# One row of condition, joined transposes and keys ahead of values in a hybrid convolution-attention layer on one core

## The chip, the cores and the metric

The kernel runs on one core of a Trainium2 chip. The metric is device time in microseconds (us) of one execution, as the median of several runs. A trace of one further execution, taken with the hardware profiler, shows what each engine did: PE (TensorE: matmuls; PEld are its weight loads), DVE (VectorE), ACT (ScalarE), POOL (GpSimd) and SP (SyncE, which here issues the DMAs).

## The reference

One layer for 512 latent tokens (a grid of 8 rows x 64 columns) and 256 context tokens, 1024 channels, all in fp32.

```python
sh, sc, gt = split(silu(c) @ w_mod + b_mod, 3)            # the condition's modulation
h  = rmsnorm(x, pre_g) * (1 + sc) + sh                    # latent tokens
hc = rmsnorm(ctx, pre_g) * (1 + sc_c) + sh_c              # context tokens, from c_ctx
b_gate, c_gate, x_in, z_a, q, k, v, z_b, g_a, g_b = split(h @ w_in)
k_c, v_c = split(hc @ w_in[:, keys and values])
q, k = rope(q), rope(k)                                   # 16 heads of 64
attn = softmax(q . [k in an 8 x 16 window, k_c] / 8 + bias) @ [v in the window, v_c]
y_a = (silu(z_a) * b_gate * conv3(c_gate * x_in)) @ w_out_conv
y_b = (silu(z_b) * attn) @ w_out_attn
y = (sigmoid(g_a) * y_a + sigmoid(g_b) * y_b) @ w_o
out = x + gt * rmsnorm(y, post_g)
```

## The kernel before, in words

Channels stand on partitions: a tensor of 512 tokens is eight tiles of 128 channels x 512 tokens. Every fp32 operand of a large matmul is split into a high and a low part (`split`, L67: ACT casts the high part, L70, DVE subtracts it from the source, L71), and a product is three matmuls, high x high, high x low, low x high (`step_T`, L115 to L117; `proj_N`, L128 and L132; `proj_c`, L140 and L144). Weights come in chunks (`Chunk`), are loaded by SP and split by ACT and DVE; the list `order` (L176) says in which order.

**The opening** (L316 to L409) is written out by hand: inside `manual_schedule` PE, DVE, ACT and SP keep the order of the code. SP loads the condition, broadcast to 128 partitions (`cb`, L317), four tiles of x (128 tokens x 1024), then per step k two slabs of the modulation weights (`wm`) and the first projection weights (`fraw`). ACT applies SiLU to `cb`. `square`, `root` and `norm` make the RMSNorm of each x tile; DVE squares tiles 0 and 1, ACT tiles 2 and 3; DVE scales tiles 0 to 2, ACT tile 3. `condition` (L260) multiplies a slab with `cb` and sums over it on DVE: half 0 gives the scale, half 1 the shift of 128 channels. PE meanwhile runs matmuls whose result nobody reads (`keep_busy`, L352) and transposes x into channels on partitions. In the loop over k (L379) ACT casts the weights (`cast_first`), DVE finishes the condition and the low part (`rest_first`), ACT modulates the transposed x (L390), `split` makes `hx`, and PE adds six projections at once (`steps`, L308 to L312).

**The middle.** After the opening a scheduler places the instructions of PE, DVE, ACT and SP, from the order of the code, the dependences, and its own estimate of durations. `turned` (L244) transposes the two context tiles for one k into a bank (banks 6 and 7 in turn) and ACT evacuates them. Convolution units follow, then `values(0)` and `keys_queries(0)` (L626). The latter projects queries and keys, applies `rope` on DVE, and writes the split operands `qd`, `qe` and `ks`. The former writes `V`.

**The attention loop** (L645) runs over 64 blocks (8 pairs of heads x 2 heads x 4 blocks of 128 queries), with projections for later pairs (`plan`, `fill`) strewn between. For block i it issues `scores` of block i + 2 (L534 or L543 on PE into bank 3 or 4; maximum with bias on DVE, L550; exponent on ACT, L557; scaling on DVE, L559, into `pt`, of which there are three buffers), then `turn` of block i: four transposes of `pt` (L565) into bank 5 or 6, and a `split` of the bank into `TH` and `TL`. After four blocks `gather` multiplies `TH` and `TL` with `V` (L580). The output stage (from L669) is not touched.

Of the kernel before, what the change touches and what calls it, by code (L numbers as in the profile page):

```python
# [9 lines left out]
F32 = mybir.dt.float32  # L10
# [17 lines left out]
def layer(ctx: ExitStack, tc, xp, ctxt, cc, wmod, small, wfirst, win, wout, wo, rel, tab, out):  # L28
# [147 lines left out]
    order = [win[i] for i in range(8)] + [vz(0, 0), qk(0)]  # L176
# [56 lines left out]
    with ExitStack() as p0:  # L233
# [10 lines left out]
        def turned(dst, xn, k):  # L244
            tp = tps()
            n = len(xn)
            for t in range(n):
                nc.tensor.transpose(tp[:, t * P:(t + 1) * P], xn[t][:, k * P:(k + 1) * P], ident)
            nc.scalar.activation(dst, tp[:, :n * P], AF.Identity, scale=sp[:, PG + k:PG + k + 1])
# [26 lines left out]

        bsc1 = const.tile([P, KT], F32, name="bsc1")
# [38 lines left out]
        with tc.manual_schedule(engines={E.PE, E.DVE, E.Activation, E.SP}):  # L316
            nc.sync.dma_start(cb[:, 0], cc[0:1].broadcast_to([P, D]))  # L317
# [6 lines left out]
            nc.vector.memset(eps, EPS)  # L324

            nc.scalar.activation(cb[:, 0], cb[:, 0], AF.Silu)
# [25 lines left out]
            def keep_busy(n, cols):  # L352

                for _ in range(n):
                    nc.tensor.matmul(acc[5][:, :cols], lhsT=ident, rhs=cb[:, 0, :cols], start=True, stop=True)

            square(0)
            square(1)
            root(0)
            norm(0)  # L360
            square(2)
            root(1)
            root(2)
            norm(1)
            norm(2)
            square(3)
            root(3)
            norm(3)
            nc.vector.tensor_scalar(out=bsc1, in0=sp[:, BM + 8:BM + 16], scalar1=1.0, scalar2=None, op0=ALU.add)
            nc.vector.tensor_scalar(out=hcv, in0=sp[:, CW:CW + 32], scalar1=0.5, scalar2=None, op0=ALU.mult)  # L370
            keep_busy(2, S)
            turned_x = {k: tps() for k in range(2)}
            for t in range(4):
                for k in range(2):
                    nc.tensor.transpose(turned_x[k][:, t * P:(t + 1) * P], xn[t][:, k * P:(k + 1) * P], ident)
                keep_busy(1, 256 if t < 3 else S)
            keep_busy(1, 256)

            for k in range(KT):  # L379
                cast_first(k)  # L380
                if k == 0:
                    condition(k, 0, [0])
                condition(k, 0, [1])
                col = cols.pop((k, 0))
                nc.vector.tensor_mul(col[:, 0:1], col[:, 0:1], sp[:, PG + k:PG + k + 1])
                rest_first(k)
                if k + 1 < KT:
                    condition(k + 1, 0, [0])
                m = st.tile([P, S], F32, name="m", bufs=2)
                nc.scalar.activation(m, turned_x.pop(k), AF.Identity, bias=col[:, 1:2], scale=col[:, 0:1])  # L390
                split(hx[0][k], hx[1][k], m)
                if k + 3 < KT:
                    load_slab(k + 3)
                    load_first(k + 3)
                elif k == 5:
                    after = Chunk(order[3])
                steps(k)
                if k + 2 < KT:
                    turned_x[k + 2] = turn_x(k + 2)
# [19 lines left out]
        for k in range(KT):  # L419
            turned(ctT[k], cn, k)  # L420
# [141 lines left out]
    def turn(pt, TH, TL):  # L562
        tp = psT().rearrange("p (c q) -> p c q", c=4)
        for c in range(4):
            nc.tensor.transpose(tp[:, c], pt[:, c * P:(c + 1) * P], ident)  # L565
        split(TH, TL, tp)
# [59 lines left out]
    for g in (values(0), keys_queries(0)):  # L626
# [15 lines left out]
    pts = {i: scores(*blocks[i]) for i in range(2)}  # L642
    T = None
    done = 0
    for i, (p, h, b) in enumerate(blocks):  # L645
# [16 lines left out]
        turn(pts.pop(i), TH[:, b], TL[:, b])  # L662
# [193 lines left out]
```

## Time and profile before

| | |
|---|---|
| median of 3 runs | 734.83 us (734.79 to 734.86) |
| the profiled execution | 737.3 us, of which the span is 733.0 us |
| PE busy | 717.9 us, 98% |
| PE weight loads busy | 598.9 us, 82% |
| DVE busy | 513.7 us, 70% |
| ACT busy | 335.1 us, 46% |
| chain that ended last | PE 94%, DVE 2%, DMA 1%, ACT 1% |
| moved by DMA | 86.09 MB, mean 117 GB/s; 344 and 405 GB/s in the first two of 40 slices |

The span is the time from the first to the last instruction; the rest of an execution lies around it. A row of the timeline has start, length, engine, line, operation, tiles (out<-in), shapes and a count, and in brackets the idle time of the engine just before, with what ended it. A matmul's row is longer than the time that it holds PE, since matmuls are pipelined: the pitch is read from one start to the next. An fp32 matmul leaves two records, an fp32r one or a transpose leaves one.

### The profile page before, as it was taken

How to read it: one execution, taken by the hardware profiler on the slowest of the kernel's cores; microseconds unless marked ns; L12 is line 12 of the kernel's file. 1: busy time of each engine (PE TensorE's matmuls, PEld its weight loads, DVE VectorE, ACT ScalarE, POOL GpSimd, SP SyncE). 2: the span in 40 equal slices, each digit the busy share in tenths (PEclk: the TensorE clock that was granted, in tenths of full speed). 3: DMA queues.
4: the chain of work that ended last, by engine and by line, in shares of the span. 5: the costliest groups of instructions: out<-in, count | busy, mean ns of one | idle time of the engine just before them, and what ended most of it. 6: DMA issues, size and time to landing. Idle time of an engine off the chain costs nothing.

```text
span 733.0 us, 9376 instructions
## 1 busy us (share of the span) xinstructions
PE 717.9 (98%) x3518; PEld 598.9 (82%) x3518; DVE 513.7 (70%) x1056; ACT 335.1 (46%) x617; POOL 0.7 (0%) x6
## 2 busy tenths in 40 slices
PE   5999999999999999999999999999999999999996
PEld 2887888788888888888888888888888888888886
DVE  6979998897897968869879778676753223234423
ACT  6575524463465544644546545534722223314321
POOL 0000000000000000000000000000000000000000
PEclk9999999999999999999999999999999999999999
DMA  9976783213122132122221212222132232234503
GB/s 344 405 264 208 278 282 114 87 44 129 58 73 72 40 104 67 65 72 72 94 94 45 93 65 72 78 81 87 58 114 83 90 115 88 85 115 147 197 1 114
DMA packets 25820, 86.09 MB, mean 117 GB/s; under 512 B 2992, under 2 KB 3376, under 8 KB 25776
## 3 DMA queue, kind: packets, MB, share of 16 engines
q1 hardware_dynamic: 25632, 85.31, 33.6%
q8 instruction: 27, 0.44, 0.2%
q10 hardware_dynamic: 144, 0.20, 0.1%
q14 instruction: 17, 0.14, 0.1%
HBM read 83.40 MB, written 2.10 MB: 117 GB/s over the span
## 4 chain that ended last, share of the span: by engine, by line
PE 94%; DVE 2%; DMA 1%; ACT 1%; issue 1%; SPq 0%; DVEq 0%; ACTq 0%
PE ps L115 20%; PE ps L116 20%; PE ps L117 20%; PE ps L128 6%; PE ps L733 6%; PE ps L580 4%; PE ps L565 4%; PE ps L132 3%; PE ps L534 3%; PE ps L308 2%; PE ps L140 2%; PE ps L309 2%; PE ps L312 1%; PE ps L543 1%; DMA x<-in_xp 1%; PE ps L144 1%
## 5 line engine op out<-in xcount | busy, mean ns | idle before, releaser
L115 PE MATMUL ps<-h,w 128*128 128x512 f32 x528 | 210.0, 398 | 0.0
L116 PE MATMUL ps<-h,w 128*128 128x512 f32 x528 | 206.2, 391 | 0.0
L117 PE MATMUL ps<-h,w 128*128 128x512 f32 x528 | 205.9, 390 | 0.0
L71 DVE TENSOR_TENSOR w<-raw,w 128x1024 fp32r<-128x1024 f32 (+1 forms) x98 | 113.4, 1173 | 61.5 <-ACT w L70 61.3
L70 ACT CAST w<-raw 128x1024 fp32r<-128x1024 f32 (+1 forms) x98 | 97.1, 1016 | 85.1 <-PE ps L117 62.8
L117 PEld LDWEIGHTS ps<-h,w 128*128 128x128 f32 x528 | 99.2, 188 | 21.3
L115 PEld LDWEIGHTS ps<-h,w 128*128 128x128 f32 x528 | 99.2, 188 | 19.6
L116 PEld LDWEIGHTS ps<-h,w 128*128 128x128 f32 x528 | 99.3, 188 | 19.2
L557 ACT ACTIVATE pt<-ps,m 128x512 f32<-128x512 f32 x64 | 44.1, 690 | 36.8 <-DVE m L554 35.8
L550 DVE CUSTOM_DVE_ANT_1 ps<-ps,bt 128x512 f32<-128x512 f32 x56 | 38.8, 695 | 17.0 <-PE ps L534 13.8
L71 DVE TENSOR_TENSOR TL<-ps,TH 128x512 fp32r<-128x512 f32 x64 | 43.5, 682 | 5.4 <-ACT TH L70 4.5
L128 PE MATMUL ps<-w,h 128*128 128x512 f32 x128 | 45.6, 398 | 0.0
L70 ACT CAST TH<-ps 128x512 fp32r<-128x512 f32 x64 | 37.1, 586 | 18.0 <-PE ps L565 17.5
L693 DVE SCALAR_TENSOR_TENSOR g<-g,ps 128x512 f32<-128x512 f32 x16 | 11.0, 686 | 39.2 <-PE ps L117 39.1
L565 PE MATMUL ps<-ident,pt 128*128 128x128 f32 x256 | 38.2, 272 | 0.0
L613 ACT ACTIVATE g<-ps 128x512 f32<-128x512 f32 x16 | 9.6, 598 | 60.3 <-PE ps L117 60.3
L565 PEld LDWEIGHTS ps<-ident,pt 128*128 128x128 f32 x256 | 31.1, 140 | 6.2 <-DVE pt L559 0.2
L132 PE MATMUL ps<-w,h 128*128 128x256 f32 x128 | 36.0, 281 | 0.0
L559 DVE TENSOR_SCALAR pt<-pt,z 128x512 f32<-128x512 f32 x64 | 30.8, 483 | 1.1
L499 ACT ACTIVATE qd<-ta 64x512 fp32r<-64x512 f32 x32 | 20.2, 631 | 18.6 <-PE ps L543 10.9
L580 PE MATMUL ps<-TH,V 128*128 128x256 f32 (+1 forms) x96 | 28.5, 319 | 0.0
L128 PEld LDWEIGHTS ps<-w,h 128*128 128x128 f32 x128 | 24.0, 188 | 5.2
(152 smaller groups left out, 1186.2 us busy)
## 6 DMA issues: line engine op xcount, KB each, us to landing
raw<-in_win SPq DMA_DIRECT2D x74, 512.0 KB, 4.1
wm<-in_wmod SPq DMA_DIRECT2D x34, 512.0 KB, 6.3
raw<-in_wout SPq DMA_DIRECT2D x16, 512.0 KB, 4.1
bt<-in_rel SPq DMA_DIRECT2D x16, 256.0 KB, 2.6
raw<-in_wo SPq DMA_DIRECT2D x8, 512.0 KB, 4.8
fraw<-in_wfirst SPq DMA_DIRECT2D x8, 384.0 KB, 8.6
x<-in_xp SPq DMA_DIRECT2D x4, 512.0 KB, 6.5
xr<-in_xp SPq DMA_DIRECT2D x4, 512.0 KB, 6.8
```

The lines of the kernel that those rows point to most:

```text
L70: nc.scalar.copy(H, src)
L71: nc.vector.tensor_sub(L, src, H.bitcast(F32))
L115: nc.tensor.matmul(ps, lhsT=H[:, k, cs], rhs=mH[k], start=k == 0, stop=False)
L116: nc.tensor.matmul(ps, lhsT=H[:, k, cs], rhs=mL[k], start=False, stop=False)
L117: nc.tensor.matmul(ps, lhsT=L[:, k, cs], rhs=mH[k], start=False, stop=k == KT - 1)
L128: nc.tensor.matmul(ps, lhsT=mH[k][:, ts], rhs=both[:, k].rearrange("p a c -> p (a c)"), start=k == 0, stop=False, skip_group_check=True,)
L132: nc.tensor.matmul(ps[:, :256], lhsT=mL[k][:, ts], rhs=H[:, k], start=False, stop=k == KT - 1, skip_group_check=True)
L550: nc.vector.tensor_tensor_reduce(out=s3, in0=s3, in1=bt[:, e::4 - e][:, 0:2], scale=1.0, scalar=-3.0e38, op0=ALU.add, op1=ALU.max, accum_o ...
L557: nc.scalar.activation(pt, s, AF.Exp, bias=m, scale=1.0, accum_out=z)
L565: nc.tensor.transpose(tp[:, c], pt[:, c * P:(c + 1) * P], ident)
L580: nc.tensor.matmul(o3[:, dst], lhsT=V[p][:, kt, h], rhs=src(t), start=n == 0 and t is TH, stop=n == len(work) - 1 and t is TL,)
L733: nc.tensor.matmul(ps, lhsT=mm[m][k][:, ts], rhs=w[k][:, cols], start=k + o == 0, stop=k == KT - 1 and o == 2)
```

## The change

1. *The condition comes as one row.* SP loads 4 KB to one partition (`crow`) in place of the broadcast. ACT applies SiLU to that row. PE spreads it over 128 partitions with a matmul against a row of ones (`spread`), 512 columns at a time, and ACT copies both halves into `cb` (`kept`).
2. *The opening's steps are moved.* Root and norm of tile 1 come before the square of tile 2; the first half of the first condition and the two small preparations (`bsc1`, `hcv`) come between the norms; `keep_busy` has 256 columns always and stands ahead of the transposes of each tile.
3. *Context transposes* are done for two k at a time: four transposes into one bank, then two evacuations.
4. *Keys and queries come first*, then values, in the list of chunks and in the code.
5. *Transposes of two blocks stand together* (`turn2`): eight transposes into both banks, then both splits. They are issued for every second block.

```diff
-    order = [win[i] for i in range(8)] + [vz(0, 0), qk(0)]
+    order = [win[i] for i in range(8)] + [qk(0), vz(0, 0)]
...
         def turned(dst, xn, k):
             tp = tps()
-            n = len(xn)
-            for t in range(n):
-                nc.tensor.transpose(tp[:, t * P:(t + 1) * P], xn[t][:, k * P:(k + 1) * P], ident)
-            nc.scalar.activation(dst, tp[:, :n * P], AF.Identity, scale=sp[:, PG + k:PG + k + 1])
+            for i in range(2):
+                for t in range(2):
+                    n = 2 * i + t
+                    nc.tensor.transpose(tp[:, n * P:(n + 1) * P], xn[t][:, (k + i) * P:(k + i + 1) * P], ident)
+            for i in range(2):
+                nc.scalar.activation(
+                    dst[i], tp[:, i * C:(i + 1) * C], AF.Identity, scale=sp[:, PG + k + i:PG + k + i + 1]
+                )
...
+        ones = const.tile([1, P], F32, name="ones")
+        crow = hp.tile([1, 2, S], F32, name="crow", tag="a0")
...
-            nc.sync.dma_start(cb[:, 0], cc[0:1].broadcast_to([P, D]))
+            nc.sync.dma_start(crow, cc[0:1].rearrange("o (a n) -> o a n", a=2))
...
-            nc.scalar.activation(cb[:, 0], cb[:, 0], AF.Silu)
+            nc.vector.memset(ones, 1.0)
+            nc.scalar.activation(crow, crow, AF.Silu)
...
-            def keep_busy(n, cols):
+            def spread(i):
+                ps = tps()
+                nc.tensor.matmul(ps, lhsT=ones, rhs=crow[:, i], start=True, stop=True)
+                return ps
+
+            def kept(i, ps):
+                nc.scalar.copy(cb[:, 0, i * S:(i + 1) * S], ps)
+
+            def keep_busy(n):
                 for _ in range(n):
-                    nc.tensor.matmul(acc[5][:, :cols], lhsT=ident, rhs=cb[:, 0, :cols], start=True, stop=True)
+                    nc.tensor.matmul(acc[5][:, :256], lhsT=ident, rhs=cb[:, 0, :256], start=True, stop=True)
+            wide = [spread(i) for i in range(2)]
             square(0)
             square(1)
+            kept(0, wide[0])
             root(0)
             norm(0)
-            square(2)
             root(1)
-            root(2)
             norm(1)
+            kept(1, wide[1])
+            square(2)
+            root(2)
+            nc.vector.tensor_scalar(out=bsc1, in0=sp[:, BM + 8:BM + 16], scalar1=1.0, scalar2=None, op0=ALU.add)
+            nc.vector.tensor_scalar(out=hcv, in0=sp[:, CW:CW + 32], scalar1=0.5, scalar2=None, op0=ALU.mult)
             norm(2)
             square(3)
             root(3)
+            condition(0, 0, [0])
             norm(3)
-            nc.vector.tensor_scalar(out=bsc1, in0=sp[:, BM + 8:BM + 16], scalar1=1.0, scalar2=None, op0=ALU.add)
-            nc.vector.tensor_scalar(out=hcv, in0=sp[:, CW:CW + 32], scalar1=0.5, scalar2=None, op0=ALU.mult)
-            keep_busy(2, S)
             turned_x = {k: tps() for k in range(2)}
             for t in range(4):
+                keep_busy(1 if t < 2 else 2)
                 for k in range(2):
                     nc.tensor.transpose(turned_x[k][:, t * P:(t + 1) * P], xn[t][:, k * P:(k + 1) * P], ident)
-                keep_busy(1, 256 if t < 3 else S)
-            keep_busy(1, 256)
+            keep_busy(3)
             for k in range(KT):
                 cast_first(k)
-                if k == 0:
-                    condition(k, 0, [0])
                 condition(k, 0, [1])
...
-        for k in range(KT):
-            turned(ctT[k], cn, k)
+        for k in range(0, KT, 2):
+            turned(ctT[k:k + 2], cn, k)
...
-    def turn(pt, TH, TL):
-        tp = psT().rearrange("p (c q) -> p c q", c=4)
-        for c in range(4):
-            nc.tensor.transpose(tp[:, c], pt[:, c * P:(c + 1) * P], ident)
-        split(TH, TL, tp)
+    def turn2(pts, b, TH, TL):
+        tps = [psT().rearrange("p (c q) -> p c q", c=4) for _ in pts]
+        for tp, pt in zip(tps, pts):
+            for c in range(4):
+                nc.tensor.transpose(tp[:, c], pt[:, c * P:(c + 1) * P], ident)
+        for n, tp in enumerate(tps):
+            split(TH[:, b + n], TL[:, b + n], tp)
...
-    for g in (values(0), keys_queries(0)):
+    for g in (keys_queries(0), values(0)):
...
-        turn(pts.pop(i), TH[:, b], TL[:, b])
+        if b % 2:
+            turn2([pts.pop(i - 1), pts.pop(i)], b - 1, TH, TL)
```

What this makes of the order of instructions is seen at three places. The first is ACT's start: SiLU, the table for the square root, then roots (`tops`, one column per tile), squares (`junka`) and the scaling of tile 3. Before:

```order
L326 ACTIVATE cb<-cb 128x1024
L327 ACT_TABLE_LOAD
L327 ACTIVATE dummy<-eps 128x1
L342 ACTIVATE tops<-tops,eps 128x1
L338 ACTIVATE junka,tops<-x_120 128x1024
L342 ACTIVATE tops<-tops,eps 128x1 x2
L338 ACTIVATE junka,tops<-x_122 128x1024
```

Now:

```order
L334 ACTIVATE crow<-crow 1x1024
L335 ACT_TABLE_LOAD
L335 ACTIVATE dummy<-eps 128x1
L366 COPY cb<-ps 128x512
L350 ACTIVATE tops<-tops,eps 128x1 x2
L366 COPY cb<-ps 128x512
L346 ACTIVATE junka,tops<-x_122 128x1024
L350 ACTIVATE tops<-tops,eps 128x1
```

The two copies into `cb` stand ahead of the square of the third tile of x, and the roots of the first two tiles stand between them.

The second is DVE ahead of the first scores: the end of the keys' rope (`ta`, `tb`), the keys (`ks`), and the first maximum (`ps,m`). Before:

```order
L467 TENSOR_TENSOR tb<-tb,cosin 128x512
L469 TENSOR_TENSOR ta<-ta,tb 128x512
L151 TENSOR_TENSOR ta<-ta,ps 128x256
L71 TENSOR_TENSOR w<-raw,w 128x4x256
L511 TENSOR_TENSOR ks<-ta,ks 64x512 x2
L511 TENSOR_TENSOR ks<-ta,ks 64x256 x2
L71 TENSOR_TENSOR w<-raw,w 128x4x256
L550 ISA ps,m<-ps,bt 128x512
```

Now:

```order
L528 TENSOR_TENSOR ks<-ta,ks 64x512 x2
L528 TENSOR_TENSOR ks<-ta,ks 64x256 x2
L151 TENSOR_TENSOR ta<-ta,ps 128x256 x2
L71 TENSOR_TENSOR V<-ta,V 128x2x64 x4
L151 TENSOR_TENSOR ta<-ta,ps 128x256
L71 TENSOR_TENSOR V<-ta,V 128x2x64 x2
L151 TENSOR_TENSOR ta<-ta,ps 128x256
L71 TENSOR_TENSOR V<-ta,V 128x2x64 x2
L151 TENSOR_TENSOR ta<-ta,ps 128x256
L71 TENSOR_TENSOR V<-ta,V 128x2x64 x2
L151 TENSOR_TENSOR ta<-ta,ps 128x256
L567 ISA ps,m<-ps,bt 128x512
```

The values' sums and splits (`V`) have come in between the keys and the first maximum.

The third is PE in the attention loop, at the end of the second head's group of four blocks: scores (`qd`, `qe`), transposes of `pt`, and the projection that follows. Before:

```order
L534 MATMUL ps<-ks,qd 128x512
L534 MATMUL ps<-ks,qe 128x512
L565 MATMUL ps<-ident,pt 128x128 x4
L534 MATMUL ps<-ks,qd 128x512
L534 MATMUL ps<-ks,qe 128x512
L565 MATMUL ps<-ident,pt 128x128 x4
L115 MATMUL ps<-h_80,w 128x512
```

Now:

```order
L551 MATMUL ps<-ks,qd 128x512
L551 MATMUL ps<-ks,qe 128x512
L551 MATMUL ps<-ks,qd 128x512
L551 MATMUL ps<-ks,qe 128x512
L583 MATMUL ps<-ident,pt 128x128 x8
L115 MATMUL ps<-h_80,w 128x512
```

Both score blocks now come first, and the transposes of two blocks stand in one run of eight.

More of the change, by code (lines that the diff above doesn't have):

```diff
@@ L350, in norm @@
                     nc.scalar.mul(xn[i], xn[i], top)
[L352 removed]
+            def spread(i):
[5 more added lines that the diff above has]
+            def keep_busy(n):
                 for _ in range(n):
[L355 removed]
+                    nc.tensor.matmul(acc[5][:, :256], lhsT=ident, rhs=cb[:, 0, :256], start=True, stop=True)
+            wide = [spread(i) for i in range(2)]
             square(0)
             square(1)
+            kept(0, wide[0])
             root(0)
             norm(0)
+            root(1)
+            norm(1)
+            kept(1, wide[1])
             square(2)
[L362 removed]
             root(2)
[L364 removed]
+            nc.vector.tensor_scalar(out=bsc1, in0=sp[:, BM + 8:BM + 16], scalar1=1.0, scalar2=None, op0=ALU.add)
+            nc.vector.tensor_scalar(out=hcv, in0=sp[:, CW:CW + 32], scalar1=0.5, scalar2=None, op0=ALU.mult)
             norm(2)
@@ L641, in layer @@
     blocks = [(p, h, b) for p in range(NPAIR) for h in range(2) for b in range(4)]
-    pts = {i: scores(*blocks[i]) for i in range(2)}
+    pts = {n: scores(*blocks[n]) for n in range(2)}
     T = None
```

## The prediction

> **What bounds the kernel now.** I read the page first, then the list of PE's waits, then the timeline of the first 17 us, then PE's rows where score blocks and transposes stand. The page:
>
> ```profile
> span 733.0 us, 9376 instructions
> ...
> PE 717.9 (98%) x3518; PEld 598.9 (82%) x3518; DVE 513.7 (70%) x1056; ACT 335.1 (46%) x617; POOL 0.7 (0%) x6
> ```
>
> PE is busy for 98% of the span, so time can only come from moments at which PE stands, or from instructions that PE starts later than it could. PE's list of waits (engine and tile, who released it, us, times, longest):
>
> ```profile
> PE ps L308 <- ACT h L70: 1.4, 1, 1.4
> PE ps L534 <- DVE ks L511: 0.6, 1, 0.6
> PE ps L534 <- ACT pt L557: 0.2, 1, 0.2
> ```
>
> The first is the end of the opening: the first real matmul waits for the first modulated input tile. The second is the first block of scores, which waits for the keys. The third is a score block whose bank is late. The opening, on the timeline (start, length, engine, what, idle before):
>
> ```profile
> 0.74 0.38 SPq L317 DMA_DIRECT2D cb<-in_cc  x1
> ...
> 5.21 1.06 ACT L326 ACTIVATE cb<-cb 128x1024 f32<-128x1024 f32 x1 [3.19 <-DMA cb<-in_cc]
> ...
> 6.41 3.75 PE L355 MATMUL ps<-cb,ident 128*128 128x512 f32 x4 [6.41 <-ACT cb L326]
> ...
> 7.74 0.29 ACT L342 ACTIVATE tops<-tops,eps 128x1 f32<-128x1 f32 x1
> 7.87 1.22 DVE L334 CUSTOM_DVE_ANT_0 junk<-x 128x1024 f32<-128x1024 f32 x1 [0.17 <-DMA x<-in_xp]
> ...
> 9.02 0.16 DVE L346 RECIPROCAL tops<-tops 128x1 f32<-128x1 f32 x1
> ...
> 9.05 1.06 ACT L338 ACTIVATE junka<-x 128x1024 f32<-128x1024 f32 x1 [1.01 <-DMA x<-in_xp]
> ...
> 10.62 0.76 DVE L348 TENSOR_SCALAR x<-x,tops 128x1024 f32<-128x1024 f32 x1
> ...
> 12.34 1.15 ACT L350 ACTIVATE x<-x,tops 128x1024 f32<-128x1024 f32 x1 [0.40 <-DVE tops L346]
> 12.40 1.28 DVE L266 CUSTOM_DVE_ANT_0 junk<-wm,cb,bsc 128x1024 f32<-128x1024 f32 x1
> ...
> 13.81 1.46 PE L355 MATMUL ps<-cb,ident 128*128 128x512 f32 x4
> 14.01 0.83 ACT L292 CAST fH<-fraw 128x768 fp32r<-128x768 f32 x1 [0.53 <-DMA fraw<-in_wfirst]
> ...
> 15.20 0.78 ACT L390 ACTIVATE m<-ps,col 128x512 f32<-128x512 f32 x1 [0.35 <-DVE col L385]
> ...
> 16.01 0.62 ACT L70 CAST h<-m 128x512 fp32r<-128x512 f32 x1
> 16.68 0.50 PE L308 MATMUL ps<-h,fH 128*128 128x512 f32 x1 [1.41 <-ACT h L70]
> ```
>
> Everything starts with loads: the broadcast condition and then four tiles of x, one after the other. DVE, ACT and loads then form one chain up to 16.68. From there PE runs nearly without a stop.
>
> **Part 1, the opening.** Rows for the loads and for the copy out of a bank: x's issue times and times to landing, the landing times of the weight chunks and of the output stores, and a 128x512 copy.
>
> ```profile
> L239 SPq DMA_DIRECT2D x<-in_xp x4: 417/428/507, 1.2 to 2.6; - x4
> ...
> DMA to landing us min/median/max: 5.3/6.5/7.7
> ```
>
> ```profile
> DMA to landing us min/median/max: 3.4/4.1/9.6
> ```
>
> ```profile
> DMA to landing us min/median/max: 1.9/2.0/2.1
> ```
>
> ```profile
> L185 ACT COPY cs<-ps x8: 581/586/588, 51.5 to 466.0; 128x512 f32<-128x512 f32 x8
> ```
>
> *Loads.* x's first tile lands at 1.2 + 5.3 = 6.5, its last at 2.6 + 7.7 = 10.3, so 1.27 us a tile. The change takes half a megabyte out of the queue ahead of them. At least one tile's spacing goes, 1.3 us. At most the first tile lands as fast as the fastest chunk, 1.2 + 3.4 = 4.6, 1.9 us earlier. I take 1.8, since that chunk too was a 512 KB load into empty queues. The second tile's square then starts at 7.87 - 1.8 = 6.1, and the reciprocal that stands at 9.02 could stand at 7.2.
>
> *The row.* Its landing has no row. The shortest landing here is 2.0 us, the broadcast's was 5.21 - 0.74 = 4.5. I take 2.0, the row of a small transfer without a queue ahead: it lands at 2.7. SiLU runs over as many elements per partition as before, 1.06, to 3.8. Two spreads are fp32 matmuls of 512 columns like the two that made 6.41's four records, 3.75 us: they end at 7.6.
>
> *The chain behind.* ACT now copies both halves into cb between the roots. The second root can start at 7.2 and takes 0.29; the second copy starts when root and spread are done, 7.7, and ends at 8.3. Then x2's square 1.06 and its accumulator read 0.2, 9.6; root 0.29, 9.9; reciprocal 0.16, 10.1; norm 0.76, 10.9. DVE now runs the first condition product ahead of the last reciprocal: 1.28 and its read, 12.3; reciprocal, 12.4; ACT's norm of x3 1.15, 13.6; cast of the first weights 0.83, 14.4 (they land at 14.0 - 1.8 = 12.2, no longer a wait); m 0.78, 15.2; h 0.62, 15.9; first matmul 16.0. That is 0.7 us earlier than 16.68, much less than the loads gain: two copies and one product have come into the chain. The second condition product on DVE, 12.4 to 13.8, is hidden behind the norm and the cast; without that cover it would be the next in line. With the loads only 1.3 us earlier the gain is 0.4; with faster spreads it is 1.0.
>
> *Clock.* The four records of 6.41 cover 2048 columns in 3.75 us, 1.83 ns a column; those of 13.81 (two of 512, two of 256 columns) take 0.95. So the PE clock comes up in between. At most 7.4 us lie between the first slow record and the first fast one that I quote. In the new order spreads, keep-busy matmuls and cold transposes stand nearly without a gap from 3.8 to about 11, and the real matmuls begin 12 us after the first spread. One gap, from about 11.5 until x3's transposes at 13.6, is longer than the 1.41 ahead of 16.68. Cost taken: nothing.
>
> The Trainium skill, TensorE: Matmul & The Clock Gate (Part 1), says that an idle stretch of about 3.4 us drops the clock; by it 2.1 us costs nothing and the sum stays. The trace shows only that 1.41 is harmless.
>
> **Part 2, context transposes.** By the order six runs on PE become three (4, 8 and 4 transposes). What a run costs is in part 4, under 0.1 us each. Taken: 0.2; between 0 and 0.5.
>
> **Part 3, keys and queries first.**
>
> ```profile
> 143.95 0.39 PE L115 MATMUL ps<-h,w 128*128 128x512 f32 x1
> 144.99 0.47 PE L534 MATMUL ps<-ks,qd 128*128 128x512 f32 x1 [0.65 <-DVE ks L511]
> ```
>
> The step is 1.04 us where an ordinary one is 0.23 (part 4): 0.8 lost. In the new order 96 value matmuls stand between the keys' last matmul and the first scores: half have 512 columns, half 256, so 48 x 0.227 + 48 x 0.114 = 16.4 us. From the first rope instruction to the last ks DVE has twenty instructions, two of them weight splits. At the 0.69 us of a 512-column one for eighteen (row in the rivals' part) and the 1.28 of a 1024-column one for two that is 15 us, and it begins before the values do, while PE still works on the keys; so the keys are some microseconds early. What is late next is nothing on PE: values are wanted only by the first gather. With the restart behind the wait I take 0.9; between 0 and 1.0.
>
> **Part 4, eight transposes in a row.** A run of four between projections, a run of four with scores behind it, and the only run of eight that there is now:
>
> ```profile
> 172.52 0.60 PE L565 MATMUL ps<-ident,pt 128*128 128x128 f32 x4
> ...
> 173.20 0.39 PE L116 MATMUL ps<-h,w 128*128 128x512 f32 x1
> ...
> 175.74 0.39 PE L115 MATMUL ps<-h,w 128*128 128x512 f32 x1
> ...
> 178.01 0.39 PE L116 MATMUL ps<-h,w 128*128 128x512 f32 x1
> ```
>
> ```profile
> 185.30 0.60 PE L565 MATMUL ps<-ident,pt 128*128 128x128 f32 x4
> ...
> 185.97 0.39 PE L534 MATMUL ps<-ks,qe 128*128 128x512 f32 x1
> ```
>
> ```profile
> 516.04 1.04 PE L565 MATMUL ps<-ident,pt 128*128 128x128 f32 x8
> ...
> 517.15 0.40 PE L116 MATMUL ps<-h,w 128*128 128x512 f32 x1
> ```
>
> Ten steps from 175.74 to 178.01 are 0.227 each; that is PE's pitch. The eleven from 173.20 to 175.74 are 0.231: a tail of 0.04. From 172.52 to 173.20 lie four transposes and one matmul, 0.68 - 0.227 = 0.45. So a run of four costs 0.49. With scores behind there is no tail: 0.67 - 0.227 = 0.44. Eight cost 1.11 - 0.227 + 0.04 = 0.92. Two runs of four joined save 0.98 - 0.92 = 0.06 where a projection followed the first, 0.93 - 0.92 = 0.01 where scores did. By the order, 62 runs of four and one of eight become two of four and 31 of eight: 30 are joined, six of them with scores behind. 24 x 0.06 + 6 x 0.01 = 1.5. If the longer run brings a longer tail it is 0.8, with the rounding of the rows up it is 1.8.
>
> The new waits: the fourth pt has three buffers, so the exponent of the newest scores waits for the run of eight. That run stands right behind those scores on PE, and their maximum on DVE takes longer than half the run; nothing waits. The last wait of PE's list, 0.2, stays, since its neighbours keep their places.
>
> **The sum.** 0.7 + 0.2 + 0.9 + 1.5 = 3.3 us. The profiled execution took 737.3 (733.0 of span and 4.3 around it); it becomes 734.0. The median of the runs is 734.83, 2.5 below the profiled one; 3.3 off gives 731.5.
>
> **Rivals.**
>
> *A late opening* (0.12). The row lands as late as the broadcast did, 2.5 us later than taken; spreads end at 10.1, the second copy at 10.7 instead of 8.3, and the first matmul stands at 18.4: 1.7 lost where 0.7 was won, 733.9. A clock that falls in the 2.1 us gap costs about as much: half the speed for some microseconds, 7.4 / 2 = 3.7 at most. For it: the row's 2.0 us is a store's. Against: 4 KB is little.
>
> *Gathers wait for two splits* (0.05). Each gather reads TH and TL of four blocks; the split of a block is a cast on ACT and a subtraction on DVE.
>
> ```profile
> 253.80 0.59 ACT L70 CAST TH<-ps 128x512 fp32r<-128x512 f32 x1
> ...
> 257.13 0.68 DVE L71 TENSOR_TENSOR TL<-ps,TH 128x512 fp32r<-128x512 f32 x1
> ...
> 259.00 0.39 PE L580 MATMUL ps<-TH,V 128*128 128x512 f32 x1
> ```
>
> ```profile
> 211.03 0.69 DVE L71 TENSOR_TENSOR TL<-ps,TH 128x512 fp32r<-128x512 f32 x1
> ...
> 212.02 0.39 PE L580 MATMUL ps<-TH,V 128*128 128x512 f32 x1
> ```
>
> The last TL is ready 1.2 us ahead of one gather, 0.3 ahead of another. Now two splits come at once at the end. If the last is 2.0 us later (0.59 + 0.68, and one more 0.69 ahead of it on DVE), a gather like the first waits 0.8; with half of the sixteen like it 6.4 us are lost, 731.5 + 6.4 = 737.9, slower. It decides from about 5 us, 0.3 a gather. Against it: DVE's list holds the same work ahead of the last TL, with the earlier TL only moved down, so the last ends about when it did.
>
> The Trainium skill, Perfetto Trace Analysis (Optimizing Tensor Performance), wants groups to rotate through banks so that one is emptied while the next is written; filling both at once goes against it. No run here shows two full banks waited for.
>
> *Joining saves nothing* (0.12): the tail after eight is as long as two tails, and the restart grows. Then 1.5 goes: 733.0. Only one run of eight speaks against it.
>
> *The keys' wait moves* (0.06): DVE's values work delays the keys or the maxima as much. Then 0.9 goes: 732.4.
>
> **How the numbers follow.** My case has 0.65, at 731.5. About 0.2%, 1.5 us, is what a measurement here tells from no change, so faster means under 733.4. My case, joining-saves-nothing, the moved wait and a quarter of the late opening are faster: 0.86. The rest of the late opening is the same: 0.09. The gathers are slower: 0.05. The range takes in the ends of the parts, 1.0 + 0.5 + 1.0 + 1.8 = 4.3 off at best, 730.5, and half a microsecond more for what I priced low, 730.0; upward it reaches over the two smaller rivals to 733.4. Outside lie the gathers, most late openings, and 0.05 below.
>
> **What would show it.** Right: the first matmul of the loop near 16.0; no wait for ks in PE's list; runs of eight transposes with a pitch of 0.227 after some ten steps; gathers without idle time. Wrong: the second copy into cb past 9 us, PE steps over 0.25 at the loop's start, idle PE ahead of gathers, or a first score row that waits.

## The result and the profile after

The changed kernel takes 731.08 us (median of 4 runs, 730.69 to 731.63); the kernel before takes 734.81 beside it (734.78 to 734.86). The ratio is 0.995 with a 95% interval of 0.9933 to 0.9967. That is 3.7 us less, and more than the 1.5 us that a measurement here can't tell from no change. The profiled execution took 731.4: 729.6 of span and 1.8 around it. The span is 3.4 shorter than before.

The page of the changed kernel, then PE's list of waits (engine and tile, who released it, us, times, longest):

```profile
span 729.6 us, 9373 instructions
...
PE 718.8 (99%) x3526; PEld 603.3 (83%) x3526; DVE 513.9 (70%) x1057; ACT 332.6 (46%) x619; POOL 0.7 (0%) x6
```

```profile
PE ps L362 <- ACT crow L334: 3.3, 1, 3.3
PE ps L395 <- ACT x L358: 0.9, 1, 0.9
PE ps L551 <- ACT pt L574: 0.4, 1, 0.4
PE ps L315 <- ACT h L70: 0.3, 1, 0.3
```

PE was 98% busy and is 99% busy. The wait for ks is gone, the wait for h fell from 1.4 to 0.3, and the wait for pt grew from 0.2 to 0.4. No gather waits.

The opening, on the timeline of the changed kernel (start, length, engine, what, idle before):

```profile
0.74 0.34 SPq L324 DMA_DIRECT2D crow<-in_cc  x1
...
2.22 1.05 ACT L334 ACTIVATE crow<-crow 1x1024 f32<-1x1024 f32 x1 [0.21 <-DMA crow<-in_cc]
...
3.33 3.78 PE L362 MATMUL ps<-crow,ones 1*128 1x512 f32 x4 [3.33 <-ACT crow L334]
...
4.39 1.23 DVE L342 CUSTOM_DVE_ANT_0 junk<-x 128x1024 f32<-128x1024 f32 x1 [3.38 <-DMA x<-in_xp]
...
7.25 0.57 ACT L366 COPY cb<-ps 128x512 f32<-128x512 f32 x1
...
8.13 1.06 ACT L346 ACTIVATE junka<-x 128x1024 f32<-128x1024 f32 x1 [0.31 <-DMA x<-in_xp]
...
10.84 1.28 DVE L271 CUSTOM_DVE_ANT_0 junk<-wm,cb,bsc 128x1024 f32<-128x1024 f32 x1
...
12.25 1.15 ACT L358 ACTIVATE x<-x,tops 128x1024 f32<-128x1024 f32 x1 [1.28 <-DVE tops L354]
13.30 0.82 ACT L299 CAST fH<-fraw 128x768 fp32r<-128x768 f32 x1
...
14.02 0.77 ACT L407 ACTIVATE m<-ps,col 128x512 f32<-128x512 f32 x1
...
14.83 0.62 ACT L70 CAST h<-m 128x512 fp32r<-128x512 f32 x1
...
15.50 0.51 PE L315 MATMUL ps<-h,fH 128*128 128x512 f32 x1 [0.32 <-ACT h L70]
```

The row has landed when SiLU starts at 2.22; the broadcast was awaited until 5.21. The chain by which the prediction worked is all there, each link 0.2 to 0.5 us ahead of its place in the sum, and the loop's first matmul stands at 15.50 in place of 16.68. But two of its links wait for loads, not for the link before: ACT's square of the third tile (8.13) for that tile, and DVE's first product of the condition (10.84) for its slab of weights, as the part on the scatter shows.

### Where the time went, by stages

A median mixes the stages, so the comparison is made between landmarks on PE: the first and the last matmul of the loop over k (L315 to L319 in the changed kernel), the first matmul of the first gather, the last of the last gather, and PE's last matmul. All values are differences of starts in the trace, in us. The names are those of the experiments below: u_ undoes or changes one thing in the changed kernel, b_ does one part alone in the kernel before.

| kernel | median us (range) | first matmul of the loop | loop | to the first gather | gathers | rest |
|---|---|---|---|---|---|---|
| before | 734.81 (734.78 to 734.86) | 16.68 | 35.56 | 117.96 | 350.22 | 206.41 |
| after | 731.08 (730.69 to 731.63) | 15.50 | 36.05 | 116.37 | 349.15 | 206.37 |
| u_join | 732.59 (732.35 to 732.88) | 15.58 | 36.07 | 116.52 | 350.19 | 206.41 |
| u_keys | 732.59 (732.13 to 732.92) | 15.13 | 36.03 | 117.48 | 349.19 | 206.36 |
| u_open | 732.00 (731.96 to 732.12) | 16.66 | 35.54 | 116.30 | 349.17 | 206.37 |
| u_ctx | 731.94 (731.21 to 732.16) | 15.74 | 36.02 | 116.83 | 349.17 | 206.36 |
| b_row | 734.04 (733.37 to 735.32) | 15.84 | 35.53 | 117.98 | 350.19 | 206.41 |
| b_moved | 735.76 (734.83 to 736.31) | 16.83 | 36.05 | 118.07 | 350.21 | 206.41 |
| u_gap | 731.62 (731.27 to 733.37) | 15.87 | 37.61 | 116.40 | 349.17 | 206.36 |
| u_ones | 731.43 (731.02 to 731.84) | 15.68 | 36.02 | 116.37 | 349.04 | 206.37 |
| u_busy | 731.49 (731.08 to 731.61) | 15.22 | 36.01 | 116.33 | 349.20 | 206.37 |
| u_wide | 731.43 (730.83 to 731.94) | 16.03 | 36.06 | 116.35 | 349.18 | 206.36 |
| u_recip | 731.31 (730.88 to 731.67) | 15.27 | 36.03 | 116.49 | 349.18 | 206.37 |
| u_place | 730.85 (730.34 to 731.27) | 15.58 | 35.54 | 116.32 | 349.17 | 206.37 |

Between the first two rows lie 1.18 won ahead of the loop, 0.49 lost in the loop, 1.59 won up to the first gather, 1.07 won among the gathers, 0.04 won behind them: 3.39, the difference of the spans. Three columns (loop, to the first gather, gathers) fall into a few clear groups each; the column of the first matmul scatters. These two facts set the experiments.

### The profile page after: what moved, and what is told of

It reads as the page before. It is cut to its first block, busy times and chain, and to the rows that moved or that the text cites. A ratio compares the mean times of both kernels' runs of the same rounds, so it can differ in the third digit from the quotient of the medians.

```text
span 729.6 us, 9373 instructions
## 1 busy us (share of the span) xinstructions
PE 718.8 (99%) x3526; PEld 603.3 (83%) x3526; DVE 513.9 (70%) x1057; ACT 332.6 (46%) x619; POOL 0.7 (0%) x6
## 4 chain that ended last, share of the span: by engine, by line
PE 94%; DVE 2%; ACT 1%; DMA 1%; SPq 0%; issue 0%; DVEq 0%; ACTq 0%
PE ps L115 20%; PE ps L117 20%; PE ps L116 20%; PE ps L128 6%; PE ps L754 6%; PE ps L599 4%; PE ps L583 4%; PE ps L132 3%; PE ps L551 3%; PE ps L140 2%; PE ps L315 2%; PE ps L319 2%; PE ps L316 2%; DMA wm<-in_wmod 1%; PE ps L560 1%; PE ps L144 1%
## 5 line engine op out<-in xcount | busy, mean ns | idle before, releaser
L70 ACT CAST TH<-ps 128x512 fp32r<-128x512 f32 x64 | 35.0, 588 | 6.6 <-PE ps L583 6.4
L583 PE MATMUL ps<-ident,pt 128*128 128x128 f32 x256 | 33.3, 272 | 0.0
L583 PEld LDWEIGHTS ps<-ident,pt 128*128 128x128 f32 x256 | 29.4, 140 | 2.2
```

The costliest lines, as they stand in the source:

```text
L70: nc.scalar.copy(H, src)
```

## The experiments

The theory after the result: the parts add up as priced, but the opening gives back some of its gain in the loop, whose period is longer than before. The rivals: joining saves nothing; the keys' wait is only moved; the opening's gain is lost later.

### Each part undone

**u_join**, part 5 undone:

```diff
-        if b % 2:
-            turn2([pts.pop(i - 1), pts.pop(i)], b - 1, TH, TL)
+        turn(pts.pop(i), TH[:, b], TL[:, b])
```

> The changed kernel with part 5 undone: one block's four transposes and their split at a time, all else as changed (median of the changed kernel 731.08 us). Theory, each run of transposes costs PE a restart and a tail and joining saves 24 of them in whole and 6 in part: 1.5 to 1.75 us come back, 732.6 to 732.8; the trace has 62 runs of four in the attention loop. Rival, joining saves nothing and the stage became shorter because the scheduler placed other work anew: within 0.3 of 731.1, and the stretch from the first scores to the last gather as long as in the changed kernel.

Measured: 732.59, and the stages show it in one place. The gathers take 350.19 as in the kernel before, 1.04 more; 0.15 more lie ahead of the first gather, 0.04 behind the last. Joining is worth 1.23 us: the rival falls. A run of eight in the changed kernel, on PE:

```profile
176.17 1.04 PE L583 MATMUL ps<-ident,pt 128*128 128x128 f32 x8
176.97 0.47 PE L115 MATMUL ps<-h,w 128*128 128x512 f32 x1
177.28 0.39 PE L116 MATMUL ps<-h,w 128*128 128x512 f32 x1
...
179.57 0.39 PE L117 MATMUL ps<-h,w 128*128 128x512 f32 x1
```

From 176.17 to 177.28 it is 1.11, as in the one run of eight before; ten steps to 179.57 are 2.29, a tail of 0.02 to 0.03. So a run was priced rightly. Part of the saving was lost at the score block that waits for pt, in the changed kernel:

```profile
202.18 0.40 PE L128 MATMUL ps<-w,h 128*128 128x512 f32 x1
202.97 0.50 PE L551 MATMUL ps<-ks,qd 128*128 128x512 f32 x1 [0.39 <-ACT pt L574]
```

That step takes 0.79; it takes 0.72 in u_join. The other 0.2 between 1.5 and 1.23 was not located.

**u_keys**, part 4 undone:

```diff
-    order = [win[i] for i in range(8)] + [qk(0), vz(0, 0)]
+    order = [win[i] for i in range(8)] + [vz(0, 0), qk(0)]
...
-    for g in (keys_queries(0), values(0)):
+    for g in (values(0), keys_queries(0)):
```

> The changed kernel with part 4 undone: values first, then keys and queries, in the list of chunks and in the code. Theory, the wait of the first scores for the keys was all that this part removed: the wait for ks is back in PE's list (0.6 us, with a step of 1.04) and the time is 0.8 to 0.9 longer, 731.9 to 732.0. Rival, the wait was only moved and comes back elsewhere in the changed kernel (a score block that waits for pt longer): the ks wait is back but another wait shrinks, and the time is within 0.3 of 731.1.

Measured: 732.59. The stage up to the first gather takes 1.11 more, and no other wait in PE's list shrinks: the rival falls. First u_keys, then the changed kernel, at the first scores:

```profile
142.50 0.39 PE L115 MATMUL ps<-h,w 128*128 128x512 f32 x1
143.53 0.47 PE L551 MATMUL ps<-ks,qd 128*128 128x512 f32 x1 [0.64 <-DVE ks L528]
```

```profile
138.59 0.28 PE L132 MATMUL ps<-w,hc 128*128 128x256 f32 x1
138.71 0.40 PE L551 MATMUL ps<-ks,qd 128*128 128x512 f32 x1
```

Of the 1.11, 0.80 is the waiting step (1.03 in place of 0.23) and 0.08 the step behind it (143.53 to 143.84 takes 0.31). Another 0.15 lies at the third score block of u_keys, at 147.30, whose weight load waits for pt: the two steps around its start take 0.27 and 0.34. The last 0.08 was not located.

**u_ctx**, part 3 undone (`turned` for one k, two transposes a bank).

> The changed kernel with part 3 undone: context transposes for one k at a time, two transposes per bank. Theory, three more runs of transposes at under 0.1 us each beside projections: 0.2 longer, 731.3, with six runs in the trace. Rival, the joined transposes made the context chain later and cost as much as they saved: 731.1 or less.

Measured: 731.94, and 0.46 in its stage, twice what I had taken. u_ctx has seven runs of context transposes, the changed kernel three. The weight loads of the transposes wait for ACT to empty a bank (lists of waits, u_ctx first, then the changed kernel):

```profile
PEld ps L248 <- ACT ctT L249: 1.2, 4, 0.4
```

```profile
PEld ps L250 <- ACT ctT L252: 0.4, 2, 0.2
```

The trace of u_ctx shows runs of two with one projection between them:

```profile
70.13 0.44 PE L248 MATMUL ps<-ident,c 128*128 128x128 f32 x2
70.33 0.48 PE L115 MATMUL ps<-h,w 128*128 128x512 f32 x1
70.64 0.38 PE L248 MATMUL ps<-ident,c 128*128 128x128 f32 x2
70.78 0.48 PE L116 MATMUL ps<-h,w 128*128 128x512 f32 x1
71.14 0.44 PE L248 MATMUL ps<-ident,c 128*128 128x128 f32 x2
```

The step from 70.33 takes 0.31, as behind the run of eight above (176.97 to 177.28); the step from 70.78 takes 0.36, since the run behind it waits for its bank. In each of the four runs whose weight load waited, the matmul before the run takes 0.03 to 0.08 longer than usual, and the first transpose takes 0.166 in place of 0.109. Together that is 0.4 of the 0.46: it is the banks that cost, much more than the restarts of four more runs.

**u_open**, parts 1 and 2 undone.

> The changed kernel with parts 1 and 2 undone: broadcast condition and the old order of the opening. Theory, the opening's 1.18 us (first matmul of the loop at 15.50 in place of 16.68) is kept but for some 0.3 that the loop over k gives back, since its period was 4.63 in place of 4.57: 0.9 longer, 732.0, first matmul at 16.7, loop period 4.57. Rival A, all of the 1.18 is kept: 732.3 with the period unchanged at 4.63. Rival B, the opening's gain is lost in later stages: within 0.3 of 731.1. The spread of the changed kernel's runs (0.9 us, where before's was 0.08) goes if the new opening makes it.

Measured: 732.00. First matmul and loop are those of the kernel before (16.66, 35.54), all later stages those of the changed one. So the opening brings 16.68 + 35.56 - 15.50 - 36.05 = 0.69 by the end of the loop, and nothing is lost behind it. The runs lie within 0.16, as before: the spread of 0.9 belongs to the new opening.

### What makes the opening scatter

In the new opening ACT squares x's third tile (`square(2)`) once it has landed, or right behind the second copy where it landed earlier, and the first matmul of the loop follows at a nearly fixed distance. u_keys, the earliest, and u_wide, the latest, each with that square and its first matmul:

```profile
7.79 1.06 ACT L346 ACTIVATE junka<-x 128x1024 f32<-128x1024 f32 x1
...
15.13 0.51 PE L315 MATMUL ps<-h,fH 128*128 128x512 f32 x1 [0.31 <-ACT h L70]
```

```profile
8.67 1.06 ACT L346 ACTIVATE junka<-x 128x1024 f32<-128x1024 f32 x1 [0.71 <-DMA x<-in_xp]
...
16.03 0.50 PE L315 MATMUL ps<-h,fH 128*128 128x512 f32 x1 [0.32 <-ACT h L70]
```

15.13 - 7.79 = 7.34 and 16.03 - 8.67 = 7.36; in the changed kernel 15.50 - 8.13 = 7.37. But in u_gap it is 7.47 and in u_join 7.56, so this tile doesn't decide alone. In u_join DVE's first product of the condition, `condition(0, 0, [0])`, waits for its slab of the modulation weights, a load that SP issues behind the tiles of x:

```profile
10.93 1.28 DVE L271 CUSTOM_DVE_ANT_0 junk<-wm,cb,bsc 128x1024 f32<-128x1024 f32 x1 [0.34 <-DMA wm<-in_wmod]
...
15.58 0.50 PE L315 MATMUL ps<-h,fH 128*128 128x512 f32 x1 [0.31 <-ACT h L70]
```

From this product to the first matmul it is 4.65 here, and 15.50 - 10.84 = 4.66 in the changed kernel. In all nine kernels with this opening (u_recip has another order) it lies between 4.65 and 4.66, and the product starts 0.02 to 0.03 behind the landing of its slab. So that landing decides. The product's start moves over 0.90, from 10.48 in u_keys to 11.38 in u_wide, as much as the changed kernel's runs differ; that the landing also makes these differ is argued from that. Medians of these kernels can so differ by some tenths for no other reason. Why the loads land at different times was not tried, nor why b_moved's runs differ by 1.5, whose slab lands as in the kernel before (11.73 and 11.72).

### What makes the loop slower

The loop's matmuls, from one start to the next, take 233 ns on average in the changed kernel, in most of the loop 229 and 238 in turn, and 229 on average with the fix that was found in the end (u_place); the step behind a run of transposes, some 315 in both, is left out. The last step over k, where u_place takes 227 for each, first in the changed kernel, then in u_place:

```profile
48.04 0.40 PE L315 MATMUL ps<-h,fH 128*128 128x512 f32 x1
48.28 0.39 PE L316 MATMUL ps<-h,fL 128*128 128x512 f32 x1
48.51 0.40 PE L315 MATMUL ps<-h,fH 128*128 128x512 f32 x1
48.75 0.39 PE L316 MATMUL ps<-h,fL 128*128 128x512 f32 x1
48.98 0.40 PE L315 MATMUL ps<-h,fH 128*128 128x512 f32 x1
```

```profile
48.18 0.39 PE L318 MATMUL ps<-h,fH 128*128 128x512 f32 x1
48.40 0.39 PE L319 MATMUL ps<-h,fL 128*128 128x512 f32 x1
48.63 0.39 PE L318 MATMUL ps<-h,fH 128*128 128x512 f32 x1
48.86 0.39 PE L319 MATMUL ps<-h,fL 128*128 128x512 f32 x1
49.08 0.39 PE L318 MATMUL ps<-h,fH 128*128 128x512 f32 x1
```

Four steps take 0.94 in the one, 0.90 in the other. The transposes between them keep 0.109 each in both, and the granted clock is 1.00 in both, so it is not the clock. Seven kernels narrowed it down.

**b_row**, the kernel before with part 1 alone (row, SiLU on it, `spread`, `kept`; the steps in the old order):

> The kernel before with part 1 alone: the condition as one row, SiLU on it, two spreads, two copies; the opening's steps otherwise in the old order. Theory, the loads are what the opening gains from: x's tiles land 1.3 to 1.9 us earlier, the first matmul of the loop stands near 15.9 (between 15.5 and 16.3) in place of 16.68, and the time is 0.4 to 1.0 shorter than 734.77. Rival, without the moved steps the copies into cb only lengthen ACT's list: first matmul at 16.5 or later, time within 0.3. On the loop over k, whose period with the new opening is 4.63 in place of 4.57: if matmuls with a single row of weights leave TensorE slower, the period is 4.63 here too; if the moved keep_busy does it, it is 4.57.

**b_moved**, the kernel before with part 2 alone:

> The kernel before with part 2 alone: the steps of the opening in the new order and keep_busy of 256 columns ahead of each tile's transposes, with the condition still broadcast. Theory, the order alone brings little: the first half of the first condition now runs while x's last tile is squared, which saves up to its 1.28 us only where DVE was late, and x lands as late as before: first matmul of the loop between 16.2 and 16.9, time within 0.5 of 734.77. Rival, the order is what gains: first matmul at 15.8 or earlier, time about 0.9 shorter. The loop's period is 4.63 if the shorter stop ahead of the loop or keep_busy's new place makes PE slower there, 4.57 if the row's matmuls do.

Measured: b_row 734.04 (ratio 0.999, 0.9981 to 0.9999), first matmul at 15.84, loop 35.53. b_moved 735.76 (1.0012, 1.0003 to 1.0022), first matmul at 16.83, loop 36.05. The loads give the gain, as the theory had it (one of b_row's 11 runs took 735.32 with a span of 732.4, like the spans of the others, so its excess lies outside the span); the moved steps alone lose 0.15 ahead of the loop, less than b_moved's runs differ, and 0.49 in it, where I had expected no effect beyond 0.5. With the row in place they do help ahead of the loop: from the landing of the first slab to the first matmul it is 4.94 in b_row and 4.68 in the changed kernel, 0.26 won against the 0.49 lost. And the slow loop comes with part 2, not with matmuls of a single row.

**u_gap**, the changed kernel without the three `keep_busy` matmuls that stand ahead of the loop:

```diff
-            keep_busy(3)
```

> The changed kernel without its last three keep_busy matmuls, which stand between the transposes of x's last tile and the loop: PE then stops for 1.5 us ahead of the loop in place of 0.3. Theory, PE's slower pitch in the loop (233 ns in place of 227 to 230, period 4.63) comes from a phase that a stop of over a microsecond resets, as the 1.4 us in the kernel before did: period 4.57, the loop 0.45 us shorter, time 730.6. Rival A, the pitch comes from elsewhere: period 4.63, time 731.1. Rival B, the clock falls in the stop: first steps of the loop at twice 0.23 and the time 1 us or more longer.

Measured: the theory falls, and rival B comes true. From the second step over k on the period is 4.63 as ever, but the clock fell at the loop's start. u_gap's matmuls and, from the windows, the granted clock (stretch, its length, busy time and count of PE, PEclk, DMA share, GB/s):

```profile
13.82 0.44 PE L395 MATMUL ps<-ident,x 128*128 128x128 f32 x2 [0.25 <-ACT x L358]
15.87 0.51 PE L315 MATMUL ps<-h,fH 128*128 128x512 f32 x1 [1.61 <-ACT h L70]
...
17.17 0.63 PE L315 MATMUL ps<-h,fH 128*128 128x512 f32 x1
17.59 0.63 PE L316 MATMUL ps<-h,fL 128*128 128x512 f32 x1
```

```profile
16.00:17.00 1.00, 1.00 (x4) 0.79 1.05 422
17.00:18.00 1.00, 1.00 (x3) 0.50 0.99 395
...
19.00:20.00 1.00, 1.00 (x4) 0.50 1.01 401
```

Steps of 0.43 in place of 0.23 cost 37.61 - 36.05 = 1.56 us. In the timed runs it shows in some and not in others: 731.27, 731.60 and 731.62, but 733.33 and 733.37. The trace is of the 733.37. So three matmuls that compute nothing were worth 1.6 us in two of five executions, the second by its time alone.

The Trainium skill, TensorE: Matmul & The Clock Gate, says in Part 1 that the clock is halved after an idle window of some 3.4 us, and that this window runs freely, whatever the kernel does. It says in Part 4 that transposes don't count as busy in the same way. The trace agrees with a window that runs freely: its record of the granted clock is at full from 13.17, at half from 16.59 and at full again from 20.00, two stretches of 3.41 us, while PE stood for no longer than 1.61. Between 13.17 and 16.59 PE ran the end of the `keep_busy` matmuls (to 13.56), two transposes and the first 0.7 us of the loop. That executions are hit or not by where the window falls is argued, from one trace of u_gap; in the traces of the other kernels with the row and the moved steps the clock comes up between 10.71 and 13.17. How busy a window has to be, and whether the transposes at 13.82 count, no run shows.

**u_ones**, the row of ones in a buffer that is free in the opening:

```diff
-        ones = const.tile([1, P], F32, name="ones")
+        ones = hp.tile([1, P], F32, name="ones", tag="hc7")
```

> The changed kernel with the row of ones kept in a buffer that is free in the opening, so that no later tile's address moves by its 512 bytes; each engine's instructions and their order are the same. Theory, addresses: the slower pitch in the loop (233 ns) comes from the operands' new places in memory: pitch 227 to 230, period 4.57, time 730.6. Rival, addresses do nothing: period 4.63 and 731.1 within the spread of the changed kernel's own runs, 730.7 to 731.6.

**u_busy**, the changed kernel with the old `keep_busy`:

> The changed kernel with keep_busy as in the kernel before (two of 512 columns ahead of the first transposes, one of 256 behind each of the first three tiles, 512 and 256 behind the last), the other steps of the opening as changed. In the runs so far the slow pitch of the loop (233 ns, period 4.63) stood wherever part 2 was in and nowhere else. Theory, keep_busy's new place and width make it: period 4.57 here, the loop 0.45 us shorter, and with the first matmul near 15.5 a time of 730.6 to 730.9. Rival A, the moved steps of DVE and ACT make it: period 4.63, time 731.1 to 731.4. Rival B, the new keep_busy was needed for the clock: steps of 0.43 us at the loop's start and over 732.

**u_wide**, `keep_busy` in the new places, 512 columns where two of 256 stood:

> The changed kernel with keep_busy in its new places, but in matmuls of 512 columns where two of 256 stood, so the same work in fewer instructions. Theory, the count of instructions ahead of the loop sets the slow pitch: period 4.57, time near 730.7. Rival A, the places set it, or steps of other engines: period 4.63 and the time of the changed kernel, 731.1 to 731.4.

**u_recip**, one step moved:

```diff
-            condition(0, 0, [0])
             norm(3)
+            condition(0, 0, [0])
```

> The changed kernel with one step moved: the reciprocal of x's last tile stands ahead of the first half of the first condition on DVE, which ACT's norm of that tile waited for (1.28 us of idle ACT). Theory, the next limit is DVE, whose two condition halves and product end as late as before, 13.6: the first matmul of the loop comes 0.1 to 0.3 us earlier, near 15.4, and the time is 730.8 to 731.3. Rival, the norm of the last tile was what the opening waited for: first matmul 1 us earlier, 14.5, time 730.2. On the pitch: if it comes from the order of DVE's steps the period is 4.57 here.

Measured: loops of 36.02, 36.01, 36.06 and 36.03. All four theories on the pitch fall. u_recip's first matmul stands 15.27 - 7.95 = 7.32 behind the square of x's third tile, against 7.37: the 1.28 us for which ACT waits at 12.25 aren't what the opening waits for. In u_recip ACT scales the last tile at 11.02, but its later steps then wait for the first weights (0.37) and for PE's transposes of that tile, and DVE's column (`col`) is ready at 13.58, no earlier than in the changed kernel (13.60):

```profile
13.79 0.78 ACT L407 ACTIVATE m<-ps,col 128x512 f32<-128x512 f32 x1 [0.41 <-PE ps L395]
```

What was left of part 2 was the order of squares, roots and norms, and one side effect. A pool gives buffers their place in the order in which the code first asks for them. With `condition(0, 0, [0])` ahead of the loop, the small `col` buffers (4 of 32 bytes) come before `fH` and `fL`: in the built program `fH` begins at byte 201632 of a partition in the changed kernel, 128 bytes further than in b_row (201504).

**u_place**, the buffers asked for first; the instructions and their order stay:

```diff
+        def place_first(k):
+            first[k] = tuple(st.tile([P, 768], F32R, name=n, bufs=3) for n in ("fH", "fL"))
+
         def cast_first(k):
-            H, L = (st.tile([P, 768], F32R, name=n, bufs=3) for n in ("fH", "fL"))
-            first[k] = H, L
-            nc.scalar.copy(H, raws[k])
+            if k not in first:
+                place_first(k)
+            nc.scalar.copy(first[k][0], raws[k])
...
+            place_first(0)
             condition(0, 0, [0])
             norm(3)
```

> The changed kernel with one thing other: the buffers of the first weights (fH and fL) get their place ahead of the small col buffers, as in the kernel before. In the new order of the opening col came first and moved fH and fL by 128 bytes. Every engine's instructions and their order are the same. What is left of part 2 for the slow pitch of the loop (233 ns) is the order of the squares, roots and norms, or these 128 bytes. Theory, the place of the weights: period 4.57, the loop (first to last matmul) 35.5 to 35.6 us in place of 36.05, and 730.6 to 731.0 with the first matmul between 15.1 and 15.7. Rival, the order of the steps: period 4.63, loop 36.05, 731.1 to 731.4.

Measured: loop 35.54, period 4.57, median 730.85 (ratio to before 0.9943, 0.9929 to 0.9957). The theory holds: 128 bytes in the place of the weights cost the loop 0.5 us. u_place has the lowest median of all kernels here; against the changed one the trace shows the 0.51 in the loop, while the medians, 0.23 apart, lie within the scatter of the opening. In the built programs of the two kernels nothing but `fH`, `fL` and `col` lies at another place, and of these PE reads only `fH` and `fL`; the two weren't moved one at a time. A shift of 512 bytes does nothing: `fH` begins at 200992 in the kernel before, 512 bytes ahead of b_row and u_place, and all three have the short loop; it begins at 201120 in b_moved and u_ones, 512 ahead of the changed kernel, and these three have the long one. By what the memory makes matmuls slower at that place stays open.

## Why the prediction was right

*Opening, 0.7.* Right in size by luck, wrong in its making: 1.18 ahead of the loop, where I had 0.7, less 0.49 in the loop, where I had nothing, is 0.69. Ahead of the loop, what I had on the loads failed. I took 1.8 off every load; x's first tile came 2.1 earlier (its square starts at 4.39 in place of 6.47), but the third tile and the first slab only 0.9 (8.13 in place of 9.05, and a landing at 10.82 in place of 11.72). The row itself landed half a microsecond earlier than taken (2.2, not 2.7), since its price came from stores, and the second copy ended at 7.8, not 8.3; but ACT then waits for the tile and DVE for the slab, so the chain through the copies that I summed is not the one that bound. From ACT's scaling of the last tile (12.25) to the first matmul it is 3.25, where I had 3.6 (12.4 to 16.0): I added lengths of rows, but the next row on ACT starts before the one ahead of it ends (the cast takes 0.72 from start to start, 13.30 to 14.02, not 0.83). In the loop, the step that failed is the pitch of PE: I had listed steps over 0.25 at the loop's start as a sign, and never priced a loop that is 1.4% longer throughout. The order of instructions shows no such thing; only the buffers' places do.

*Clock, nothing.* Right, but the cover is thinner than I had it: u_gap shows the `keep_busy` matmuls between x's last transposes and the loop to be what keeps the clock. I had looked at the longer gap ahead of those transposes.

*Context transposes, 0.2.* Mis-sized: 0.46 by u_ctx, near the upper bound of 0.5. I had priced the restarts of runs alone. What I left out are the waits of the transposes for banks that ACT hadn't emptied, 0.4 of the 0.46; the kernel before has them too (its weight loads wait 1.2 us there, five times).

*Keys first, 0.9.* Mis-sized: 1.11 by u_keys. The wait's 0.8 is there (142.50 to 143.53 is 1.03); the step behind it and the third score block, which was late too, add 0.23 where I had added 0.1.

*Eight transposes, 1.5.* 1.23 by u_join. The run of eight cost what was taken. "The last wait of PE's list, 0.2, stays" failed: it became 0.4 (a step of 0.79 in place of 0.72). That the exponent there now waits for a whole run of eight would explain it, but was not tried; some 0.2 more was not located.

*The sum.* 0.69 + 0.46 + 1.11 + 1.23 = 3.5, against 3.3 predicted and 3.4 between the spans: two terms too small, one too large. The four parts were undone one at a time, and what they cost by stages adds up within 0.1, so no more than that comes of one part acting on another. By the medians the four cost 4.8 together, against the 3.7 gained: the scatter of the opening is in the changed kernel's median, from which each is taken. The rivals: no late opening, no gather that waits, the joining does save, and the keys' wait didn't move.

## What to carry to other kernels

Take an average apart by landmarks on the bounding engine: the runs of the changed kernel scatter by 0.9 us, about as much as the landing of a load moves, while stage lengths repeat within 0.2 and show which part does what. When steps are moved, see whether buffers moved too: the order in which code asks a pool for them sets their addresses. Matmuls without a use that stand ahead of a first real one can be worth more than they seem, and one should be sure before one takes them out.

## What the runs showed of the hardware that I had not expected

- Matmuls of 512 columns in a loop ran at 233 ns on average in place of 229 when their weights' buffers lay 128 bytes further on, with the same instructions and a granted clock of 1.00 (changed kernel and u_place); 512 bytes changed nothing (u_ones).
- The clock fell to 0.50 for 3.41 us, after 3.41 us at full speed in which PE stood for 1.61 us at a stretch (u_gap, the traced execution), while 1.41 ahead of the loop in the kernel before never did harm.
- Transposes into two banks in turn, two at a time, cost 0.4 us in waits for ACT to empty the banks (u_ctx).
- A 4 KB row was there 2.2 us into the span, 1.5 after its issue began; a broadcast of the same row to 128 partitions took 4.5.
